# A decoder layer in split fp32 products: few keys' weights scaled three times for one transpose per head, the values' weights split among the keys, and a row sum moved ahead

## The chip, the core and the metric

The kernel runs on one core of one Trainium2 chip. The metric is device time in us, the median of several runs of the program. The engines are TensorE (PE: matmuls, transposes, with a queue PEld that loads the stationary operand), VectorE (DVE), ScalarE (ACT), GpSimd (POOL) and SyncE (SP, which here issues transfers). Each engine works through its own instructions in a fixed order and waits by semaphores.

## The reference

One layer over T = 272 tokens (16 meta tokens ahead of 256) of width D = 2048:

```python
p = h @ w_in                      # q (8 heads x 128) | c_kv (256) | q_idx (16 x 64) | k_idx (64) | w_idx (16) | u (1024)
c_kv = rms_norm(c_kv, g)
score = einsum(relu(q_idx . k_idx), w_idx)      # causal; each query keeps its 64 best keys
logits = (q absorbed by w_uk) . c_kv * 128**-0.5 + T5 bias      # of the keys kept
attn = softmax(logits) @ c_kv, then through w_uv per head
pool = (trailing means of u over 2, 4, 8, 16 minus u) @ w_pool per group, scaled
h = layer_norm(alpha * h + concat(attn, pool) @ w_o)
z = causal depthwise conv of width 3 over h @ w_up
out = layer_norm(alpha * h + (gelu(a) * g) @ w_down)      # a, g the halves of z; meta tokens dropped
```

All inputs and the output are fp32.

## The kernel before

**Products.** Every fp32 factor is held as two parts, hi (an ACT copy rounded to fp32r, L127) and lo (the rest, a DVE subtraction, L128). Each product is three matmuls into one PSUM bank: hi·hi, hi·lo and lo·hi (L199 to L201 in `product`, and the like elsewhere).

**Weights.** They come as a `stream` of tiles of 1 MB, in the order of use. `emit` (L135) takes the next: `fetch` (L110) issues its transfer on SP and splits it in two halves of 1024 columns on ACT and DVE. `weights` (L165) hands out the next tile after it has emitted two more ahead of it (three raw buffers, three split ones). `behind` and `tc.issue_after` add edges to the program, by which an instruction is issued behind another on its engine. The rest of the order is the framework's scheduler's: it puts the instructions of each engine in a fixed order. PSUM has two pools of four banks: `small()` (shown as `at`) and `big()` (shown as `mm`).

**The stages,** with their place in the profiled span:

1. *Warm-up* (L85 to L89): POOL sets a bf16 tile, then 13 matmuls on it. They write nothing that is used.
2. *First products* (L264 to L270): index key, index weights and latent KV, 16 slices k, each split as it lands (L222 to L225). Three PSUM tiles ("heads"), for each k three matmuls for one, then for the next.
3. *Index queries* (to about 82 us): eight products; ACT and DVE evict each into a query tile (L383, L384). `dots` (L352) multiplies it with the key (L358, L359), ACT applies relu from PSUM, DVE adds up the weighted scores.
4. *Keys and values* (75 to 93 us): eight keys `kt` = w_uk times the latent (L398 to L400, evicted on ACT at L401), the last dots among them at key 2; then `few` and the values `v0` (first 16 keys), `v1`, `v2` from w_uv (L409 to L439). `few` holds hi and lo of the latent of the first 16 keys in rows 0 and 32 of a stationary operand of 48 columns, so one product gives both; `v0` has 80 rows: hi, lo and hi again at 0, 32 and 64.
5. *Heads* (138 to 211 us): the products of q and the pool channels. For each head a softmax (L489), `turn` (L504), which transposes the weights (three of 128x128 and, for the first 16 keys, two of 128x16, L506 to L510) and builds `ptx` with the rows hi, hi, lo of these few keys' weights, and `values` (L523). The 16 meta tokens' last two queries have their own small softmax (L463 to L483, tile `lm`), transposed by eight small transposes.
6. *Output product, layer norm, FFN* (to about 1009 us): w_o, w_up and w_down, in part with sums of four blocks in the place of eight products.
7. *Tail* (L895 to L1016): the last four tiles of w_down are applied, `spare` (split tile `whl_y`), `spare` + 1, `spare` + 2 (both `whl`) and the last, which is fetched and split ahead of them into small tiles `whl_r`. Each is taken column by column, in `pieces` of 512 or 256, the one from 1792 to 2048 with two more columns. These hold the row sums of the weights, so that the mean of the second layer norm comes out of the same product. `row_sums` (L185): ACT copies a raw tile onto itself with an accumulated sum (L188), rounds it (L190), DVE takes the rest (L191). Those of `spare`, + 1 and + 2 run behind the split of `spare` + 2, and so do the sums of y (L915). The y adds (L843) close the last parts of the FFN's products.

In the profile L991 to L993 are the tail's matmuls, L785 to L787 and L837 to L839 the FFN's.

## Time and profile before

| what | value |
|---|---|
| median of 3 runs | 1043.34 us (1043.13 to 1043.67) |
| profiled execution | 1043.2 us, of which 1041.3 are the profile's span |
| granted TensorE clock | 0.998 |
| busy: PE, DVE, ACT, POOL | 1033.3, 891.0, 621.0, 189.5 us |
| matmuls | 7643 |
| read from HBM | 232.50 MB, 225 GB/s over the span |

A timeline row has the start (us from the span's start), the busy time, the engine, the line, the operation, output<-input, the shapes and how many instructions it holds; in brackets the idle time just before and what ended it. Consecutive matmuls overlap: a start to the next start is the time that one takes from PE, not its duration. A row of a group has busy us and mean ns of one, then the idle time before it. In the list of waits the numbers are us in total, times, and the longest.

### The profile page before, as it was taken

Reading aid. Unit: us, or ns where it says so; the run is one execution under the profiler, and the core shown is the slowest. Engines: PE = TensorE matmul, PEld = TensorE weight load, DVE = VectorE, ACT = ScalarE, POOL = GpSimd, SP = SyncE. Lnnn points to the kernel's source line nnn. Section 1 sums busy time; section 2 is a strip of 40 time slices with the busy share of each in tenths; the row PEclk is TensorE's granted clock in tenths of the full one; section 3 lists DMA queues with packets and bytes.
Section 4 is the critical chain, followed back from the end, with each engine's and each line's share of the span. In section 5 each row is a group of like instructions: output and inputs, shape, how many; then the busy total and the mean of one; then the engine's idle time right before and its main releaser. Section 6 shows DMA issues by size and latency. Waiting matters only on the chain.

```text
span 1041.3 us, 19198 instructions
## 1 busy us (share of the span) xinstructions
PE 1033.3 (99%) x7643; PEld 984.3 (95%) x7643; DVE 891.0 (86%) x1401; ACT 621.0 (60%) x1000; POOL 189.5 (18%) x246
## 2 busy tenths in 40 slices
PE   9999999999999999999999999999999999999997
PEld 9999999999999999999999999999999999999986
DVE  6879568758779998888999999989998999999876
ACT  7656446645439855555665556555556565565665
POOL 1200014125330021130121111211112101120031
PEclk9999999999999999999999999999999999999999
DMA  9755543354553578879887788877988778887865
GB/s 326 259 187 218 214 142 131 134 200 165 176 189 131 197 223 240 278 282 302 274 277 261 269 297 276 276 263 267 296 271 285 264 274 285 279 273 271 288 215 160
DMA packets 59754, 250.28 MB, mean 240 GB/s; under 512 B 21734, under 2 KB 22416, under 8 KB 32656
## 3 DMA queue, kind: packets, MB, share of 16 engines
q1 hardware_dynamic: 34592, 230.42, 61.2%
q0 software_dynamic: 7888, 16.14, 8.3%
q10 hardware_dynamic: 17184, 2.49, 1.4%
q8 instruction: 60, 0.98, 0.4%
q14 instruction: 30, 0.25, 0.1%
HBM read 232.50 MB, written 2.11 MB: 225 GB/s over the span
## 4 chain that ended last, share of the span: by engine, by line
PE 89%; DVE 5%; issue 3%; ACT 1%; POOL 1%; DMA 1%; POOLq 0%; DVEq 0%; ACTq 0%
PE mm L200 22%; PE mm L199 22%; PE mm L201 22%; PE at L786 6%; PE at L785 6%; PE at L787 6%; DVE whl L128 2%; DMA wraw<-in_w_down 1%; PE mm L268 1%; PE mm L269 1%; PE mm L270 1%; ACT whl L127 1%; DVE x L701 0%; DVE hp L706 0%; PE at L358 0%
## 5 line engine op out<-in xcount | busy, mean ns | idle before, releaser
L128 DVE TENSOR_TENSOR whl<-wraw,whl 128x1024 fp32r<-128x1024 f32 (+1 forms) x416 | 486.3, 1203 | 37.7 <-ACT whl L127 36.8
L127 ACT ACTIVATE whl<-wraw 128x1024 fp32r<-128x1024 f32 (+1 forms) x416 | 402.8, 1015 | 98.6 <-PE mm L201 21.7
L200 PE MATMUL mm<-hp,whl 128*128 128x258 f32 x1280 | 362.4, 283 | 0.1
L199 PE MATMUL mm<-hp,whl 128*128 128x258 f32 x1280 | 361.4, 282 | 0.0
L201 PE MATMUL mm<-hp,whl 128*128 128x258 f32 x1280 | 361.2, 282 | 0.0
L200 PEld LDWEIGHTS mm<-hp,whl 128*128 128x128 f32 x1280 | 242.7, 190 | 3.3 <-DVE hp L706 0.3
L199 PEld LDWEIGHTS mm<-hp,whl 128*128 128x128 f32 x1280 | 242.5, 189 | 3.3
L201 PEld LDWEIGHTS mm<-hp,whl 128*128 128x128 f32 x1280 | 242.9, 190 | 0.2
L199 PE MATMUL mm<-xp,whl 128*128 128x256 f32 (+5 forms) x384 | 111.9, 291 | 0.0
L200 PE MATMUL mm<-xp,whl 128*128 128x256 f32 (+5 forms) x384 | 108.7, 283 | 0.0
L201 PE MATMUL mm<-xp,whl 128*128 128x256 f32 (+5 forms) x384 | 108.7, 283 | 0.0
L720 ACT ACTIVATE z<-mm,cv 128x256 f32<-128x256 f32 x40 | 22.6, 564 | 100.9 <-PE mm L201 100.9
L757 POOL TENSOR_TENSOR forms<-za 128x128 f32<-128x128 f32 x20 | 21.9, 1095 | 309.6 <-DVE za L738 243.1
L720 ACT ACTIVATE za<-mm,cv 128x256 f32<-128x256 f32 x40 | 22.6, 565 | 85.5 <-PE mm L201 77.4
L199 PEld LDWEIGHTS mm<-xp,whl 128*128 128x128 f32 x384 | 72.4, 189 | 1.0 <-issue 0.5
L200 PEld LDWEIGHTS mm<-xp,whl 128*128 128x128 f32 x384 | 72.3, 188 | 0.4
L201 PEld LDWEIGHTS mm<-xp,whl 128*128 128x128 f32 x384 | 72.4, 189 | 0.3 <-DVE whl L128 0.2
L786 PE MATMUL at<-whl,gp 128*128 128x512 f32 x180 | 71.1, 396 | 0.0
L787 PE MATMUL at<-whl,gp 128*128 128x512 f32 x180 | 71.0, 395 | 0.0
L785 PE MATMUL at<-whl,gp 128*128 128x512 f32 x180 | 69.3, 395 | 0.0
L760 POOL TENSOR_TENSOR forms<-za 128x128 f32<-128x128 f32 x20 | 22.6, 1131 | 199.0 <-DVE za L738 185.4
L787 PEld LDWEIGHTS at<-whl,gp 128*128 128x128 f32 x180 | 33.8, 188 | 7.9
(348 smaller groups left out, 1918.2 us busy)
## 6 DMA issues: line engine op xcount, KB each, us to landing
wraw<-in_w_up SPq DMA_DIRECT2D x88, 1024.0 KB, 5.0
wraw<-in_w_down SPq DMA_DIRECT2D x80, 1024.0 KB, 6.2
wraw<-in_w_proj SPq DMA_DIRECT2D x24, 1024.0 KB, 5.1
wraw<-in_w_o SPq DMA_DIRECT2D x16, 1024.0 KB, 4.9
y<-v POOLq DMA_DIRECT2D x27, 256.0 KB, 8.2
y<-u POOLq DMA_DIRECT2D x18, 256.0 KB, 4.9
wraw<-in_w_first SPq DMA_DIRECT2D x8, 304.0 KB, 5.4
x<-in_xt SPq DMA_DIRECT2D x1, 2176.0 KB, 8.4
```

The lines of the kernel that those rows point to most:

```text
L127: upper = nc.scalar.activation(hl[:, 0, c], raw[:, c], AF.Copy)
L128: lower = nc.vector.tensor_tensor(hl[:, 1, c], raw[:, c], hl[:, 0, c].bitcast(F32), op=ALU.subtract)
L199: nc.tensor.matmul(ps, wh, ah, start=n == 0, stop=False)
L200: nc.tensor.matmul(ps, wh, al, start=False, stop=False)
L201: nc.tensor.matmul(ps, wl, ah, start=False, stop=n == KT - 1)
L268: nc.tensor.matmul(ps[:m, :T], wh, x_parts[k][:, 0, :], start=k == 0, stop=False)
L720: nc.scalar.activation(z, src[:, 2:NQ], AF.Identity, bias=col(C_B, j), scale=col(C_W, 3 * j + 2))
L757: nc.gpsimd.tensor_tensor(s[:, 0], a21, a22, op=ALU.add)
L760: nc.gpsimd.tensor_tensor(s[:, 3], a11, a21, op=ALU.subtract)
L785: nc.tensor.matmul(ps, a[:, 0, i], hl[:, 0, w], start=j == 0, stop=False)
L786: nc.tensor.matmul(ps, a[:, 0, i], hl[:, 1, w], start=False, stop=False)
L787: nc.tensor.matmul(ps, a[:, 1, i], hl[:, 0, w], start=False, stop=j == n - 1)
```

## The change

Six edits, all in one kernel; the products and their order on PE stay as they were but for what is named here.

1. **Start.** The warm-up reads a constant of ones in the place of a tile that POOL sets, with 14 matmuls for 13. In the first products the three PSUM tiles' hi·hi go first for k < 4, then their hi·lo, then their lo·hi.
2. **Values' weights.** w_uv is fetched by its turn in the stream but not split there; its raw and split tiles are kept in `held`. Its two halves are split behind the evictions of keys 1 and 3. The evictions of the keys are issued behind the last query's. The last dots use the big PSUM buffers. The tile after w_uv in the stream, the first of the heads' products, is split where w_uv was.
3. **Few keys' values.** `few` has 48 dense columns (hi, hi, lo), `v0` has 112 rows; ACT writes 32 rows at once, POOL copies 48 rows to 64.
4. **Few keys' weights.** The softmax scales the weights of the first 16 keys apart, three copies side by side into a tile `fews` for both blocks of queries (48 columns each, at 0 and 64), so one transpose of 112 columns takes the place of two. The result's parts are formed by row: `lower_row` is 1 for the rows that are to hold lo and 0 for the others; ACT copies with scale 1 − 2·lower_row, so hi or −hi, and DVE adds lower_row times the full value.
5. **Meta queries' weights.** `lm3` holds three copies of `lm` (two DVE copies), eight transposes of 48 columns for 16; the parts in the same way, in `pm_parts`, from which POOL copies two columns per head into `ptx`.
6. **Tail.** The row sum of `spare` is issued when `spare` + 1 is emitted, behind `spare`'s split and ahead of `spare` + 1's. The two others follow the split of `spare` + 2 as before; the sums of y are issued behind them.

By the programs' orders, DVE now does both last y adds (L843; L887 in the changed kernel) between the low halves of `spare` + 1 and those of `spare` + 2; before, it did one ahead of each of the latter's two. On PE one matmul of the tail's second piece goes ahead of the first that needs the low half of `spare` + 2. PE has 8 transposes fewer and one warm-up matmul more. SP's transfers and their order are the same.

```diff
-    warm = sb.tile([P, 256], mybir.dt.bfloat16, name="warm")
-    nc.gpsimd.memset(warm, 0.0)
+    warm = nc.const_aps.tensor(1.0, (P, 256), mybir.dt.bfloat16)
     ps = small()
-    for _ in range(13):
+    for _ in range(14):
...
+    def split_part(raw, hl, c, after=()):
+        with ExitStack() as edges:
+            for ins in after:
+                edges.enter_context(tc.issue_after(ins))
+            upper = nc.scalar.activation(hl[:, 0, c], raw[:, c], AF.Copy)
+        lower = nc.vector.tensor_tensor(hl[:, 1, c], raw[:, c], hl[:, 0, c].bitcast(F32), op=ALU.subtract)
+        return tuple(getattr(ins, "ins", ins) for ins in (upper, lower))
...
+        if i == VALUES:
+
+            nc.sync.dma_start(raw, stream[i])
+            held.extend((raw, hl))
+            return
+        if i == spare + 1:
+
+            with behind(spare):
+                sums = row_sums(spare, ready[spare])
+            split[i] = fetch(raw, hl, stream[i], None, 0, (sums,))
...
+        terms = [(t, h) for h in heads for t in range(3)]
+        if k < 4:
+            terms.sort(key=lambda x: x[0])
...
-        nc.scalar.activation(kt[:, h, :], ps[:, :T], AF.Copy)
+        with tc.issue_after(query):
+            key = nc.scalar.activation(kt[:, h, :], ps[:, :T], AF.Copy)
         if h == 2:
-            dots(7, qis[7], small(), (0, 1))
+            dots(7, qis[7], big(), (0, 1), big)
+        if h in (1, 3):
+
+            split_part(*held, slice(512 * h - 512, 512 * h + 512), (getattr(key, "ins", key),))
...
+        nc.scalar.activation(v[:32, w], ps[:32], AF.Copy)
+        nc.vector.tensor_tensor(low, ps[:NM], v[:NM, w].bitcast(F32), op=ALU.subtract)
+        nc.vector.tensor_tensor(low, ps[32:48], low.bitcast(F32), op=ALU.add)
+        nc.gpsimd.tensor_copy(v[64:FEW, w], v[:48, w])
...
+    def stacked_parts(to, ps, r):
+
+        nc.scalar.activation(to, ps, AF.Copy, scale=lower_row[r:r + 48, 1:2])
+        nc.vector.scalar_tensor_tensor(to, ps, lower_row[r:r + 48, 0:1], to.bitcast(F32), op0=ALU.mult, op1=ALU.add)
...
-            nc.vector.tensor_scalar_mul(lg[:, a:b], lg[:, a:b], st[:, 2, i:i + 1])
+            nc.vector.tensor_scalar_mul(lg[:, a + NM:b], lg[:, a + NM:b], st[:, 2, i:i + 1])
+            nc.vector.tensor_scalar_mul(fews[h % 2][:, 64 * i:64 * i + 48].rearrange("p (a b) -> p a b", b=NM),
+                                        lg[:, None, a:a + NM].to_broadcast([P, 3, NM]), st[:, 2, i:i + 1])
...
-        nc.tensor.transpose(ptm[:NM, :P], lg[:, :NM], ident)
-        nc.tensor.transpose(ptm[:NM, P:2 * P], lg[:, KA:KA + NM], ident)
+        nc.tensor.transpose(ptm[:FEW, :P], fews[h % 2], ident)
...
-        for r in (0, 32):
-            nc.vector.tensor_copy(ptx[r:r + NM, :2], pm_sb[:, h, :])
-            nc.scalar.activation(ptx[r:r + NM, 2:], ptm[:NM, :2 * P], AF.Copy)
-        nc.vector.tensor_tensor(ptx[64:64 + NM, :2], pm_sb[:, h, :], ptx[:NM, :2].bitcast(F32), op=ALU.subtract)
-        nc.vector.tensor_tensor(ptx[64:64 + NM, 2:], ptm[:NM, :2 * P], ptx[:NM, 2:].bitcast(F32), op=ALU.subtract)
+        nc.gpsimd.tensor_copy(ptx[:48, :2], pm_parts[:, h, :])
+        for i in range(2):
+            stacked_parts(ptx[64 * i:64 * i + 48, 2 + P * i:2 + P * i + P], ptm[64 * i:64 * i + 48, :P], 64 * i)
...
     with behind(spare + n - 2):
-        for k in range(n - 1):
-            row_sums(spare + k, hls[k])
+        for k in range(1, n - 1):
+            of_weights = row_sums(spare + k, hls[k])
...
     for i in range(2):
-        nc.scalar.activation(y2[:, i], y2[:, i], AF.Copy, accum_out=mvs[i][:, 0:1])
+        with tc.issue_after(of_weights):
+            nc.scalar.activation(y2[:, i], y2[:, i], AF.Copy, accum_out=mvs[i][:, 0:1])
```

More of the change, by code (lines that the diff above doesn't have):

```diff
@@ L154, in emit @@
             raw, hl = weight_tiles()
[L155 removed]
         ready[i] = hl
+        if i == VALUES:
[6 more added lines that the diff above has]
+            split[i] = fetch(raw, hl, stream[i], None, 0, (sums,))
+        else:
+            split[i] = fetch(raw, hl, stream[i], kinds.get(i), i and i - 1 in split and split[i - 1][1])
         if i >= spare:
```

92 lines of the change are left out of this document (50 added, 42 removed).

## The prediction

> **What bounds the kernel now.** I read the busy times on the page first, then the chain that ended last by engine, then what TensorE (PE) sat idle for.
>
> ```profile
> PE 1033.3 (99%) x7643; PEld 984.3 (95%) x7643; DVE 891.0 (86%) x1401; ACT 621.0 (60%) x1000; POOL 189.5 (18%) x246
> ...
> PE 89%; DVE 5%; issue 3%; ACT 1%; POOL 1%; DMA 1%; POOLq 0%; DVEq 0%; ACTq 0%
> ```
>
> And PE's list of waits, whole (us in total, times, longest):
>
> ```profile
> PE at L975 <- ACT diag L973: 1.5, 1, 1.5
> PE at L89 <- POOL warm L86: 1.1, 1, 1.1
> PE mm L992 <- DVE whl L191: 0.2, 1, 0.2
> ```
>
> PE is busy 99% of a span of 1041.3 us, and its list of waits holds 2.8 us in all (1.5 + 1.1 + 0.2). So the change can win only what it takes from PE's own work, or from short stalls that this list counts as busy. It can lose without such a bound: each us by which an operand is late for PE is a us of the end. I therefore follow PE's starts, and ask at each touched place whether the next start comes earlier or later. The usual pace is 0.12 us for 258 columns (1018.89 to 1019.01 in the last fence of this part) and by its columns 0.125 for 272 and 0.23 to 0.24 for 512.
>
> **The change, part by part**
>
> *Start.* The warm-up loses its wait for POOL's memset, gets a 14th matmul, and the first four k take all three heads' hi·hi products first.
>
> ```profile
> 1.10 2.95 PE L89 MATMUL at<-warm 128*128 128x256 bf16 x13 [1.10 <-POOL warm L86]
> ...
> 5.96 0.33 PE L270 MATMUL mm<-xp,whl 128*128 128x272 f32 x1
> ...
> 8.36 0.43 ACT L222 ACTIVATE xp<-wraw 128x272 fp32r<-128x272 f32 x1 [0.96 <-DMA wraw<-in_w_first]
> ...
> 9.20 0.51 DVE L225 TENSOR_TENSOR whl<-wraw,whl 128x336 fp32r<-128x336 f32 x1
> ...
> 9.76 0.35 PE L270 MATMUL mm<-xp,whl 128*80 128x272 f32 x1
> 9.95 0.29 PE L268 MATMUL mm<-xp,whl 128*128 128x272 f32 x1
> ```
>
> Products run at half pace until about 5.96. But at 9.76 PE takes the fifth k's low half of the weights, which VectorE (DVE) ends at 9.20 + 0.51 = 9.71; that one came through ScalarE (ACT) from a transfer that ACT had awaited until 8.36. The next start is at 9.95, 0.19 later where the pace is 0.125: PE is already waiting for data there, by some 0.06 us. Whatever it wins before 9.7 is spent in this wait, which only grows. I cost the whole edit at 0; the cover is the transfer behind 8.36. What PE loses before 9.7 isn't covered, since it has no slack there. The full pace comes 4.86 us after the first warm matmul (5.96 − 1.10). If it came 2 us later by the clock, 2 us more at half pace would cost 1 us. Bounds: −0.1 to +1.
>
> The Trainium skill, "TensorE: Matmul & The Clock Gate", section "What's actually happening", says that the clock is released by a free-running window of about 3.4 us of activity, and that the number of cold matmuls differs from run to run. The trace's 4.86 us fits one such window begun at a phase of its own. By that rule a start that is earlier on PE need not release the clock earlier, and this can go either way; my sum has 0 here by the row at 9.20, whichever holds.
>
> *Values' weights split among the keys; last dots in the big buffers.* The rows of PE, then of ACT and DVE, around 80 us:
>
> ```profile
> 80.09 0.28 PE L200 MATMUL mm<-xp,whl 128*128 128x258 f32 x1
> 80.39 0.39 PE L201 MATMUL mm<-xp,whl 128*128 128x258 f32 x1
> 80.62 0.28 PE L199 MATMUL mm<-xp,whl 128*128 128x258 f32 x1
> 81.04 0.39 PE L358 MATMUL at<-kidx,qi 128*128 128x272 f32 x1
> 81.27 0.29 PE L359 MATMUL at<-kidx,qi 128*128 128x272 f32 x1
> ...
> 85.71 0.39 PE L426 MATMUL at<-whl,few 128*48 128x512 f32 x1
> ```
>
> ```profile
> 79.51 1.06 ACT L127 ACTIVATE whl<-wraw 128x1024 fp32r<-128x1024 f32 x1
> 80.59 0.98 ACT L401 ACTIVATE kt<-at 128x272 f32<-128x272 f32 x3
> 81.44 0.31 ACT L361 ACTIVATE rl<-at 128x144 f32<-128x144 f32 x1
> ```
>
> ```profile
> 79.11 1.23 DVE L128 TENSOR_TENSOR whl<-wraw,whl 128x1024 fp32r<-128x1024 f32 x1 [0.53 <-ACT whl L127]
> 80.37 0.43 DVE L384 TENSOR_TENSOR qi<-mm,qi 64x256 fp32r<-64x256 f32 x1
> ```
>
> From 80.09 to 81.27 PE makes four steps in 1.18 us where 0.485 would do: a hidden stall of **0.70 us**. It waits for the low half of the next projection's weights (DVE 79.11 + 1.23 = 80.34), then for a PSUM buffer: the small ones hold keys that ACT evicts only at 80.59, behind the split at 79.51 that takes 1.06. In the changed order that projection is split some 6 us earlier, two keys go ahead of the first half of the values' weights, and the dots take buffers of the other pool. So both reasons go. What is late next is the relu of the first head's dots, which frees nothing before it has gone through ACT. ACT's order is then: second query (behind no split now, it ends at an estimated 78.9), two keys (2 × 0.33, to 79.5), half a split (1.0, to 80.5), a key (0.33) and the relu (0.31, to about 81.1); PE without a stall could go on at 80.97: 0.16 us of it stays. Gain 0.70 − 0.16 = **−0.53** (rounded); bounds −0.2 (a second wait of 0.3) and −0.76 (no stall at all, and the short steps around). The second half of the values' low parts comes at about 84.5 and PE, which multiplies with it at 85.71 now, wants it at about 85.3 once the stall is shorter, so 0.8 us covers the later split; if DVE were late by more, the excess would be paid.
>
> For the first values (48 stacked rows) PE keeps eight matmuls. ACT loses two of its four copies, POOL gets two of 48x512; their reader is the first head's product at 151.6 (quoted next), over 60 us later.
>
> *One transpose per head.* PE's product that reads the new tile, then PE's start of the first head and what DVE does around it:
>
> ```profile
> L526 PE MATMUL at<-ptx,v x8: 279/284/287, 151.6 to 209.3; 80*128 80x258 f32 x8
> ```
>
> ```profile
> 145.37 0.34 PE L482 MATMUL at<-ident,lm 2*16 2x2 f32 x8
> 145.65 0.33 PE L506 MATMUL at<-ident,lg 128*128 128x128 f32 x1
> ...
> 146.03 0.27 PE L509 MATMUL at<-ident,lg 128*16 128x128 f32 x1
> 146.14 0.27 PE L510 MATMUL at<-ident,lg 128*16 128x128 f32 x1
> ```
>
> ```profile
> 144.84 0.27 DVE L476 TENSOR_TENSOR lm<-lm,mmeta 2x128 f32<-2x128 f32 x1
> ...
> 145.82 0.15 DVE L483 COPY pm_sb<-at 16x16 f32<-16x16 f32 x1
> ```
>
> A transpose lasts 0.27 us, but the next starts 0.11 later (146.03 to 146.14): they overlap, and one less per head is worth 0.109 us, eight times **−0.87**. The first head alone gets something ahead: DVE has two more copies of 2x128 (0.15 each by the copy at 145.82) and two narrow scalings, which by the rows end near 145.6 where PE wants to start at 145.6: 0 to +0.1. On DVE the softmax's scalings get narrower (128 and 256 columns for 144 and 272) and two of 128x48 join; three tiny copies and one of 256 columns become two of 128: about even. ACT's two copies have 128 columns for 256. POOL's extra copy of 48x2 per head stands right behind its memset, ahead of the pool's windows; it takes 0.15 us or so, and PE reads the tile at 151.6, 5 us after the first head's transposes. I take −0.87, bounds −0.95 to +0.1.
>
> The Trainium skill, "TensorE: Matmul & The Clock Gate", section "Part 4: PE-mode transpose", gives about 275 ns for a transpose in a kernel. The trace's duration agrees (0.27), its starts don't (0.11); by the page's figure as a cost, eight would be an estimated 2.2 us.
>
> *The row sum in ACT's gap.* PE's stall that it is aimed at, and ACT's and DVE's tail:
>
> ```profile
> 1011.88 0.39 PE L992 MATMUL mm<-whl,gp 128*128 128x512 f32 x1
> ...
> 1018.89 0.28 PE L993 MATMUL mm<-whl,gp 128*128 128x258 f32 x1
> 1019.01 0.28 PE L991 MATMUL mm<-whl,gp 128*128 128x258 f32 x1
> 1019.49 0.39 PE L992 MATMUL mm<-whl,gp 128*128 128x258 f32 x1 [0.20 <-DVE whl L191]
> 1019.72 0.28 PE L993 MATMUL mm<-whl,gp 128*128 128x258 f32 x1
> ```
>
> ```profile
> 1006.43 2.02 ACT L127 ACTIVATE whl<-wraw 128x1024 fp32r<-128x1024 f32 x2 [2.83 <-DMA wraw<-in_w_down]
> ...
> 1014.67 1.90 ACT L188 ACTIVATE wraw<-wraw 128x2048 f32<-128x2048 f32 x1
> ...
> 1018.55 0.19 ACT L190 ACTIVATE whl<-total 128x2 fp32r<-128x2 f32 x1
> ```
>
> ```profile
> 1002.69 2.36 DVE L128 TENSOR_TENSOR whl_y<-wraw,whl_y 128x1024 fp32r<-128x1024 f32 x2 [1.95 <-ACT whl_y L127]
> ...
> 1009.81 0.68 DVE L843 TENSOR_TENSOR y<-y,mm 128x512 f32<-128x512 f32 x1
> 1010.40 1.22 DVE L128 TENSOR_TENSOR whl<-wraw,whl 128x1024 fp32r<-128x1024 f32 x1
> ```
>
> The last matmuls wait for the last total (1018.55 + 0.19, then DVE): 1018.89 to 1019.72 hold 0.83 us where three steps need 0.36, so 0.47 us go. In their place: the moved sum writes over the raw tile, so it waits for DVE's last low half of that tile, 1002.69 + 2.36 = 1005.05. It takes 1.90 as its like at 1014.67, and with its read-out and the two columns' copy (0.19 a row, partly overlapped) 2.15 or so; the next tile's split, now issued behind it, starts at about 1007.2 instead of 1006.43. DVE's two low halves of that tile then run 8.32 to 10.6 (us past 1000). In the changed order DVE does both adds to y next (0.60 each from start to start, 9.81 to 10.40), to 11.8, and only then the last tile's first low half (1.22): ready at 1013.02. Before, one add stood ahead of it and it was ready at 1011.62 for PE's 1011.88. One matmul that is moved ahead gives 0.23, so PE comes to it at 1012.10: a **new stall of 0.92**, with the semaphore's way 0.97. Net tail −0.47 + 0.97 = **+0.50**. Bounds: −0.47 (the tile comes early enough) and +1.5 (another us from the transfer or from the adds, which wait for PE). The remaining sums run on ACT behind the last split as before, one fewer of them, and PE asks for their totals at 1019.49 only.
>
> **Sum**: 0 − 0.53 − 0.87 + 0.50 = **−0.90**. DVE's rows that stand in between don't absorb it, since PE's chain is continuous through the FFN. The profiled execution took 1043.2 (span 1041.3 and 1.9 around it): 1042.3. The median of the runs shown is 1043.34, 0.14 above it, which gives **1042.4**.
>
> **The rivals**
>
> *A. The tail does as it is meant.* If the last tiles are ready a us earlier than I work out, or PE comes a us later to them, the new stall is nothing: −0.53 − 0.87 − 0.47 = −1.87, 1041.5. For it: the whole stall hangs on 1 us between three engines. Against: DVE's order is fixed, and 8.32 + 2.3 + 1.2 + 1.2 is a sum of measured durations. With the keys' stage at its other bound too (−0.76) it is 1041.2, just faster.
>
> *B. The moved sum delays the splits by more, slower.* Place: ACT between 1005 and 1009. The sum decides when the low half of the tile ahead of it is later than about 1004.2 (1006.43 − 2.2); from there each us costs PE one. With that transfer's landing 3.2 us later, the stall would be 4.2 and the sum −0.53 − 0.87 − 0.47 + 4.2 = +2.3: 1045.6. Against: its start at 1002.69 follows from a stream that is ahead of PE here.
>
> *C. The stall among the dots only moves* (the change doesn't do what it says): the relu or the values' low half takes the place of the split, and 0.7 stays: −0.87 + 0.50 = −0.37, 1043.0.
>
> *D. A dropped transpose gives back its duration* of 0.27, not the distance of 0.11, because PE can't overlap one with the matmul behind it: 8 × 0.27 = 2.16 for 0.87, so −2.19 in all: 1041.15. The starts at 146.03 and 146.14 speak against it. [...]
>
> *E. The clock comes later at the start*, up to +1: 1043.4.
>
> **How the numbers follow.** A measurement of this kernel can tell about 0.2%, 2.1 us, from no change, so faster means below 1041.25 and slower above 1045.4. Forecast 0.46; A 0.23, of which 0.08 lie below the bound; B 0.06, of which 0.04 lie above; C 0.14; D 0.03, all faster; E 0.08, 0.01 of it slower. Faster: 0.08 + 0.03 + 0.02 from the forecast's own spread = 0.13; slower 0.05; same 0.82. The range takes in A, C, D and E: from 1040.9 (A with the keys' −0.76, the heads' −0.95 and the start's −0.1 gives 1041.1, and 0.2 for the median's own scatter) to 1044.1 (the tail at +1.5 and the keys at −0.2 give 1043.8, and a third of E). What is left out is B and a later mix of the losses, some 1 in 10 to 2 in 10.
>
> **What would show it.** Right: between 79.9 and 81.3 PE's steps are 0.12 but for one; one transpose of 112 rows a head, its neighbour 0.11 later; the matmul at 1019.49 follows without a gap; PE has a gap of about 1 us near 1012, waiting for DVE's low half, behind two adds. Wrong: no gap there (then A); a gap above 2 us (B); PE waits for ACT's relu or DVE's low half between 80 and 86 (C); PE at half pace beyond 6.5 us (E); PE waits for the stacked weights' tile in any head, which I cost at nothing.

## The result and the profile after

The changed kernel takes 1047.40 us (median of 6 executions, 1046.95 to 1049.11) against 1043.62 for the kernel before, run beside it: ratio **1.0039, interval 1.0028 to 1.0049**. That is some 4 us slower, where 0.9 us faster was forecast and 1044.1 was the upper end of the range. The profiled execution took 1047.3, of which 1045.5 are the span; the granted clock is 0.998 as before.

The page of the changed kernel, busy times and then the chain that ended last by engine:

```profile
PE 1033.1 (99%) x7636; PEld 983.3 (94%) x7636; DVE 893.5 (85%) x1406; ACT 620.7 (59%) x999; POOL 191.2 (18%) x257
...
PE 82%; DVE 9%; issue 3%; ACT 2%; DMA 1%; POOL 1%; SPq 0%; POOLq 0%; DVEq 0%; ACTq 0%
```

PE is busy for 0.2 us less than before, in a span that is 4.2 us longer. So PE's work hardly changed and its waiting did; in the chain DVE's share rose from 5% to 9%. Among PE's waits (us in total, times, longest) three are new, beside one of 1.2 us in the start:

```profile
PE at L615 <- DVE mixa L575: 2.2, 2, 1.3
...
PE mm L1037 <- DVE whl L116: 0.9, 1, 0.9
...
PE at L556 <- DVE mixp L621: 0.7, 1, 0.7
```

`mixa` (two waits) and `mixp` are all among the heads; the whl of L1037 is the tail's wait that was forecast. What PE waits for in them is no data but a PSUM bank: DVE's subtraction into `mixa` (or `mixp`) is the last to read a head's result (or a pool group's) from a small bank, and PE's next product into that bank can't start before it. No term of the prediction names these.

**Where the 4.1 us come from.** I split the span at points that both kernels have. The heads go from the first product of the meta queries' logits to the first FFN product, before and then after:

```profile
139.01 0.45 PE L466 MATMUL at<-kt,qt 128*2 128x16 f32 x12
...
350.12 0.28 PE L199 MATMUL mm<-hp,whl 128*128 128x258 f32 x1
```

```profile
138.96 0.50 PE L494 MATMUL at<-kt,qt 128*2 128x16 f32 x14
...
352.85 0.28 PE L219 MATMUL mm<-hp,whl 128*128 128x258 f32 x1
```

211.11 us became 213.89: **+2.78**, where −0.87 was forecast. Ahead of them the two kernels are even (139.01 and 138.96). Behind them 0.63 us are lost in the FFN with no wait to be seen (measured below), and the tail, up to its last product, loses 0.75 (0.82 up to the span's end).

**The heads' first wait.** PE, before and after, at a pool product between the heads, which needs such a bank:

```profile
171.49 0.28 PE L571 MATMUL at<-df,wpl 128*128 128x258 f32 x1
```

```profile
170.82 0.28 PE L617 MATMUL at<-df,wpl 128*128 128x258 f32 x1
172.37 0.39 PE L615 MATMUL at<-df,wpl 128*128 128x258 f32 x1 [1.27 <-DVE mixa L575]
```

By its pace PE would have gone on at 170.94 (170.82 + 0.12) and it does at 172.37: 1.43 us lost. Two more follow, 1.06 at 190.5 and 0.90 at 205.8. Now ACT some 7 us earlier, before and after:

```profile
163.91 0.74 ACT L518 ACTIVATE ptx<-at 16x256 fp32r<-16x256 f32 x2
...
165.27 2.00 ACT L127 ACTIVATE whl<-wraw 128x1024 fp32r<-128x1024 f32 x2
```

```profile
164.50 0.35 ACT L521 ACTIVATE ptx<-at,lower_row 48x128 fp32r<-48x128 f32 x1
...
165.63 0.36 ACT L521 ACTIVATE ptx<-at,lower_row 48x128 fp32r<-48x128 f32 x1 [0.47 <-DVE ptx L522]
...
166.44 2.01 ACT L115 ACTIVATE whl<-wraw 128x1024 fp32r<-128x1024 f32 x2
```

Before, ACT's two copies into `ptx` ran back to back. Now the second waits for DVE's addition into the first's half of the same tile. The bracket shows only 0.47 us of waiting, but it is a wait across two queues: that addition stands behind what DVE does ahead of it. DVE, after:

```profile
165.09 0.26 DVE L547 TENSOR_SCALAR few_of<-lg,st 128x48 f32<-128x48 f32 x1
165.26 0.33 DVE L522 SCALAR_TENSOR_TENSOR ptx<-at,lower_row,ptx 48x128 fp32r<-48x128 f32 x1
...
167.53 2.94 DVE L116 TENSOR_TENSOR whl<-wraw,whl 128x1024 fp32r<-128x1024 f32 x2 [1.15 <-ACT whl L115]
...
171.90 0.42 DVE L575 TENSOR_TENSOR mixa<-at,mixa 128x258 fp32r<-128x258 f32 x1
```

And `mixa` before:

```profile
170.80 0.41 DVE L531 TENSOR_TENSOR mixa<-at,mixa 128x258 fp32r<-128x258 f32 x1
```

Read them in order: the addition ends at 165.59, so ACT's second copy at 165.63, so its weight split at 166.44 and not at 165.27 (+1.17), so DVE's low half, which had waited 1.15 for it, at 167.53, so the subtraction into `mixa` at 171.90 and not at 170.80 (+1.10). Before, `mixa`'s subtraction freed the bank at 171.21 for PE's 171.49: a margin of **0.28 us**. PE itself comes 0.55 earlier (170.94 for 171.49): four transposes are dropped by then, 4 × 0.109 = 0.44, and it began 0.05 earlier. 1.10 + 0.55 − 0.28 = 1.37 of the 1.43. So at this place the other engines, not PE, set the pace, though PE is busy 99% of the span.

POOL has a part in this chain too. Its windows (the trailing sums of the pool channels) read a tile that ACT writes behind the second copy, so they also end a us later. POOL, before and after:

```profile
166.22 2.18 POOL L553 TENSOR_TENSOR win<-win 128x263 f32<-128x263 f32 x2
```

```profile
167.20 2.19 POOL L597 TENSOR_TENSOR win<-win 128x263 f32<-128x263 f32 x2
```

DVE's last low half ends some 1.1 us behind them in both: 166.35 + 3.14 = 169.49 behind 168.40 before, 170.47 behind 169.39 after. Whether ACT's split or POOL's windows made it late can't be told from these two kernels; the next runs say more.

**The tail.** PE, then DVE, then ACT, after:

```profile
1015.22 0.39 PE L1036 MATMUL mm<-whl_y,gp 128*128 128x512 f32 x1
1016.50 0.50 PE L1037 MATMUL mm<-whl,gp 128*128 128x512 f32 x1 [0.90 <-DVE whl L116]
```

```profile
1006.14 2.36 DVE L116 TENSOR_TENSOR whl_y<-wraw,whl_y 128x1024 fp32r<-128x1024 f32 x2 [2.02 <-ACT whl_y L115]
...
1014.03 1.28 DVE L887 TENSOR_TENSOR y<-y,mm 128x512 f32<-128x512 f32 x2
1015.23 2.35 DVE L116 TENSOR_TENSOR whl<-wraw,whl 128x1024 fp32r<-128x1024 f32 x2
```

```profile
1008.53 1.92 ACT L207 ACTIVATE wraw<-wraw 128x2048 f32<-128x2048 f32 x1 [1.48 <-DVE whl_y L116]
1010.68 3.90 ACT L115 ACTIVATE whl<-wraw 128x1024 fp32r<-128x1024 f32 x4
```

The moved sum starts when DVE ends `whl_y`'s low half (1006.14 + 2.36 = 1008.50), and the next split comes 2.15 later. Two additions stand ahead of the last low half on DVE, and PE waits for that: step 1.28 where 0.23 is the pace. The old wait for the last total is gone: at the product that had it PE's step is now 0.12. All of this is as forecast.

### The profile page after: what moved, and what is told of

It reads as the page before. It is cut to its first block, busy times and chain, and to the rows that moved or that the text cites. A ratio compares the mean times of both kernels' runs of the same rounds, so it can differ in the third digit from the quotient of the medians.

```text
span 1045.5 us, 19194 instructions
## 1 busy us (share of the span) xinstructions
PE 1033.1 (99%) x7636; PEld 983.3 (94%) x7636; DVE 893.5 (85%) x1406; ACT 620.7 (59%) x999; POOL 191.2 (18%) x257
## 3 DMA queue, kind: packets, MB, share of 16 engines
HBM read 232.50 MB, written 2.11 MB: 224 GB/s over the span
## 4 chain that ended last, share of the span: by engine, by line
PE 82%; DVE 9%; issue 3%; ACT 2%; DMA 1%; POOL 1%; SPq 0%; POOLq 0%; DVEq 0%; ACTq 0%
PE mm L220 20%; PE mm L219 20%; PE mm L221 20%; PE at L829 6%; PE at L830 6%; PE at L831 6%; DVE whl L116 4%; PE mm L291 2%; DMA wraw<-in_w_down 1%; ACT whl L115 1%; ACT lg L543 0%; DVE x L745 0%; DVE hp L750 0%; DVE lg L546 0%; DVE lg L539 0%
## 5 line engine op out<-in xcount | busy, mean ns | idle before, releaser
L801 POOL TENSOR_TENSOR forms<-za 128x128 f32<-128x128 f32 x20 | 21.2, 1061 | 311.9 <-DVE za L782 245.3
L804 POOL TENSOR_TENSOR forms<-za 128x128 f32<-128x128 f32 x20 | 19.8, 990 | 200.0 <-DVE za L782 200.0
```

Source lines behind the costliest of these rows:

```text
L801: nc.gpsimd.tensor_tensor(s[:, 0], a21, a22, op=ALU.add)
L804: nc.gpsimd.tensor_tensor(s[:, 3], a11, a21, op=ALU.subtract)
```

## The experiments

Each kernel was run with the kernel before on the same chip; the ratio has its 95% interval. "Heads" is the length from the first to the second mark above, less the 211.11 of before. "FFN" is measured in the same way between two rows quoted with the reversed turn. Both come from one profiled execution of each kernel; the ten kernels that have the heads of before lie within 0.07 us of it.

| kernel | median us | ratio to before | heads | FFN |
|---|---|---|---|---|
| changed | 1047.40 | 1.0039 (1.0028 to 1.0049) | +2.78 | +0.63 |
| e1 heads as before | 1044.75 | 1.0011 (1.0003 to 1.0020) | −0.04 | +0.63 |
| e2 copies first | 1045.25 | 1.0017 (1.0008 to 1.0026) | +0.61 | +0.65 |
| e4 heads' edits alone | 1046.52 | 1.0029 (1.0017 to 1.0040) | +2.74 | 0.00 |
| e7 the wait alone | 1046.48 | 1.0030 (1.0018 to 1.0041) | +3.17 | 0.00 |
| e13 e2, small copy on DVE | 1046.74 | 1.0027 (1.0016 to 1.0037) | +2.82 | +0.63 |
| e15 e2, scalings on POOL | 1047.57 | 1.0039 (1.0025 to 1.0053) | +0.85 | +0.63 |
| e16 e4, copies first, scalings on POOL, big dots | 1044.52 | 1.0020 (1.0011 to 1.0028) | +2.83 | 0.00 |
| e5 e2, y adds late | 1044.13 | 1.0006 (0.9997 to 1.0015) | +0.14 | +0.63 |
| e9 e1, y adds late | 1044.23 | 1.0003 (0.9994 to 1.0012) | −0.06 | +0.63 |
| e10 start alone | 1043.72 | 1.0000 (0.9991 to 1.0009) | 0.00 | 0.00 |
| e14 start and tail, adds late | 1043.51 | 0.9999 (0.9990 to 1.0008) | +0.01 | 0.00 |
| e8 split and big dots alone | 1043.84 | 1.0000 (0.9991 to 1.0009) | −0.06 | +0.63 |
| e11 big dots alone | 1043.40 | 0.9994 (0.9985 to 1.0004) | +0.01 | +0.01 |
| e12 split alone | 1043.97 | 1.0004 (0.9995 to 1.0013) | −0.04 | +0.64 |
| e17 turn reversed alone | 1044.26 | 1.0008 (0.9999 to 1.0017) | −0.06 | +0.63 |
| e18 e12, turn put back | 1044.06 | 1.0005 (0.9997 to 1.0014) | 0.00 | 0.00 |
| e19 e9, turn put back | 1043.21 | 0.9992 (0.9983 to 1.0001) | +0.01 | 0.00 |
| e20 e5, turn put back | 1043.53 | 0.9995 (0.9986 to 1.0004) | +0.56 | +0.01 |

### The heads

My theory on seeing the traces: the wait between ACT and DVE in `ptx` costs the heads. The rival: it is the added work on DVE (or on POOL), and the wait is only where it shows.

**e1**: the heads and the few keys' values as before, the rest of the change kept.

```diff
-            nc.vector.tensor_scalar_mul(fews[h % 2][:, 64 * i:64 * i + 48]...
-        nc.tensor.transpose(ptm[:FEW, :P], fews[h % 2], ident)
+        nc.tensor.transpose(ptm[:NM, :P], lg[:, :NM], ident)
+        nc.tensor.transpose(ptm[:NM, P:2 * P], lg[:, KA:KA + NM], ident)
```

> The changed kernel with everything that concerns the few keys put back (stacked latent of 48 columns with gaps, values of 80 rows, one small softmax copy, two transposes per head, the copies into the tile ptx as before); start, split of the values' weights among the keys, and tail stay changed. By the trace of the changed kernel against before, PE is level with before when the heads start (139.3 in both) and 2.8 us late after them (212.2 against 209.4), and 4.1 late at its last product. Theory (the heads' part costs 2.8): about 1044.6, no gaps of a us on PE between 165 and 206 us. Rival (the stalls among the heads come from what is ahead of them, the values' weights being split later): the gaps stay, about 1047.

**e2**: the change, with both copies ahead of both additions, so that ACT waits for DVE in no head.

```diff
-        for i in range(2):
-            stacked_parts(ptx[64 * i:64 * i + 48, 2 + P * i:2 + P * i + P], ptm[64 * i:64 * i + 48, :P], 64 * i)
+        for to, low, sign in ends:
+            nc.scalar.activation(to, low, AF.Copy, scale=sign[:, 1:2])
+        for to, low, sign in ends:
+            nc.vector.scalar_tensor_tensor(to, low, sign[:, 0:1], to.bitcast(F32), op0=ALU.mult, op1=ALU.add)
```

> The changed kernel with one edit: in each head both ScalarE copies into ptx stand ahead of both VectorE additions, so the second copy no longer waits for the first addition. Nothing else is moved or left out. Theory 1 (the wait: ScalarE's second copy waits for VectorE, which first scales the next head's weights, and the weight split behind it is late by 0.5 us a head until PE has to wait): the three stalls on PE (1.4, 1.1, 0.9 us) go, about 1044.0, and the profile has ACT idle for less than 0.1 ahead of the second copy. Theory 2 (VectorE's own added work, two more scalings of 128x48 a head, makes it late): the stalls stay within a third, 1046.5 or more. Theory 3 (GpSimd's copy of 48x2, 0.8 us, holds ptx back): no change, 1047.4.

**e4**: the kernel before with the few keys' edits alone, parts 3 to 5 of the change (and the constant of ones with 13 matmuls).

```diff
-        nc.tensor.transpose(ptm[:NM, :P], lg[:, :NM], ident)
-        nc.tensor.transpose(ptm[:NM, P:2 * P], lg[:, KA:KA + NM], ident)
+        nc.tensor.transpose(ptm[:FEW, :P], fews[h % 2], ident)
```

> The kernel before with only the few keys' part of the change (and the warm-up's constant tile in the place of the one that GpSimd sets, to make room; 13 matmuls). Start order, values' weights, tail as before. If the heads' part costs its 2.8 us by itself: 1043.5 + 2.8 = 1046.3, with stalls on PE between 165 and 206. If it does so only together with the values' weights' later split: 1043.5 - 0.9 = 1042.7.

**e7**: the kernel before, its operations all kept and only put in an order that makes ACT's second copy wait for DVE.

```diff
-            nc.scalar.activation(ptx[r:r + NM, 2:], ptm[:NM, :2 * P], AF.Copy)
...
+        nc.scalar.activation(ptx[:NM, 2:], ptm[:NM, :2 * P], AF.Copy)
         nc.vector.tensor_tensor(ptx[64:64 + NM, 2:], ptm[:NM, :2 * P], ptx[:NM, 2:].bitcast(F32), op=ALU.subtract)
+        nc.scalar.activation(ptx[32:32 + NM, 2:], ptm[:NM, :2 * P], AF.Copy)
```

> The kernel before with one edit in each head: the second ScalarE copy into ptx stands behind VectorE's subtraction that ends ptx, so ScalarE waits there for VectorE, as in the changed kernel; the work is the same. Theory 1 (that wait is the cost): slower, about 1045.5, with PE stalls of 0.5 to 1.5 us among the later heads. Theory 2 (the added work): 1043.5 within 0.5.

With the heads undone (e1) their length is that of before and 2.65 us of the median go (1047.40 to 1044.75). The heads alone (e4) cost the same on the kernel before. The wait alone (e7), with no work added anywhere, costs 3.17 in the heads; and without it (e2) 2.17 of the 2.78 go, 2.15 by the medians. So the cost of ACT's wait is shown from both sides, for 2.2 us of it. PE's waits in e7, those among the heads:

```profile
PE at L572 <- DVE mixa L532: 1.6, 2, 0.8
PE at L509 <- DVE mixp L578: 0.8, 1, 0.8
```

They are at the same three places as in the changed kernel. ACT's copies and its split in e2:

```profile
164.40 0.73 ACT L565 ACTIVATE ptx<-at,lower_row 48x128 fp32r<-48x128 f32 x2
...
165.88 2.00 ACT L115 ACTIVATE whl<-wraw 128x1024 fp32r<-128x1024 f32 x2
```

The copies are back to back again. But counted from the first mark (138.72 here) the copies come 0.78 later than in the kernel before (25.68 us for 24.90) and the split 0.90 later (27.16 for 26.26), and one wait of PE for `mixa` stays, a step of 1.41 us over the pace. It is the first of the three: 1.43 in the changed kernel, and it ends 33.41 us after the first mark in both. So the order of the copies costs the second wait and the third. The first stays without it, though that order alone is enough for a wait there too (0.94 in e7). 0.61 − 1.41 = −0.80: the transposes do give what was forecast (−0.87), and the wait that is left takes it away and more. For that rest the rival may hold: the added work on DVE is in the groups of the changed kernel's heads (busy us, mean ns of one, idle time ahead):

```profile
L522 DVE SCALAR_TENSOR_TENSOR ptx<-at,lower_row,ptx 48x128 fp32r<-48x128 f32 x16 | 5.5, 347 | 2.7 <-ACT ptx L521 2.5
L547 DVE TENSOR_SCALAR few_of<-lg,st 128x48 f32<-128x48 f32 x16 | 4.1, 254 | 0.0
```

Those that they replace, in the kernel before:

```profile
L520 DVE TENSOR_TENSOR ptx<-at,ptx 16x256 fp32r<-16x256 f32 x8 | 3.3, 410 | 0.1
L517 DVE CAST ptx<-pm_sb 16x2 fp32r<-16x2 f32 x16 | 2.5, 154 | 0.2
L519 DVE TENSOR_TENSOR ptx<-pm_sb,ptx 16x2 fp32r<-16x2 f32 x8 | 1.2, 152 | 0.3
```

The additions and the copies for the few keys take 5.5 + 4.1 us for 3.3 + 2.5 + 1.2: 2.6 us more, or 0.33 a head, on a loop with 0.28 us of margin. Narrowing the wide scaling from 272 to 256 columns saved nothing (370 ns for 354).

Three tries to take the rest of e2's wait away. **e13** has POOL's copy of 48x2 on DVE, **e15** the two narrow scalings on POOL, **e16** is e4 with the copies first, these scalings on POOL and the big dots.

```diff
-        nc.gpsimd.tensor_copy(ptx[:48, :2], pm_parts[:, h, :])
+        nc.vector.tensor_copy(ptx[:48, :2], pm_parts[:, h, :])
```

```diff
-            nc.vector.tensor_scalar_mul(fews[h % 2][:, 64 * i:64 * i + 48]...
+            nc.gpsimd.tensor_scalar_mul(fews[h % 2][:, 64 * i:64 * i + 48]...
```

> The changed kernel with both ScalarE copies first in each head, and the copy of two columns (48x2) per head made by VectorE in the place of GpSimd. With the copies first, one stall of 1.4 us was left at 170.6 us, where PE waits for VectorE's subtraction of the third head's mix. Theory A (what is left is VectorE's own added work, 0.24 us a head by its starts): the stall grows, to 1.6 to 2, since VectorE gets 0.1 us more per head; 1045.4. Theory B (GpSimd's copy is what is left: it delays the windows that VectorE waits for): the stall falls under 0.7; 1044.5.

> The changed kernel with both ScalarE copies first in each head, and the two scalings of 128x48 per head made by GpSimd in the place of VectorE. With the copies first alone, 1.4 us of stall was left at 170.6 us and the kernel took 1045.25. Theory (VectorE's added scalings, 0.34 us a head by their starts, are what is left): the stall falls under 0.6, and the heads' stage is shorter than before's 211.1 us by 0.3 or more; 1044.3. Rival (GpSimd's work delays its windows, or holds VectorE, by as much): the stall stays above 1.2, 1045.2 or more.

> The kernel before with the few keys' part (copies first, the narrow scalings on GpSimd), the warm-up's constant tile, and the last dots in the big buffers; values' weights and tail as before. A candidate for a version better than both. Theory: 1043.6 - 0.3 (dots) - 0.4 (heads) = 1042.9. Rival (a stall among the heads takes it back): 1043.6 or more.

None did: the one step is 2.15 in e13, 1.73 in e15 and 2.11 in e16. In e15 DVE now waits 0.27 us for POOL's scalings.

What is left of the wait has POOL's windows in its chain. DVE in e2, ahead of the second head's `mixa` and then in the third head, and POOL there:

```profile
162.43 0.43 DVE L606 SCALAR_TENSOR_TENSOR diff<-win,u 128x258 f32<-128x258 f32 x1 [0.73 <-POOL win L600]
...
166.97 3.26 DVE L116 TENSOR_TENSOR whl<-wraw,whl 128x1024 fp32r<-128x1024 f32 x2 [0.57 <-ACT whl L115]
```

```profile
166.97 2.18 POOL L600 TENSOR_TENSOR win<-win 128x263 f32<-128x263 f32 x2
```

The second head's windows end 0.79 us later after the first mark than in the kernel before (23.68 us for 22.89), DVE waits 0.73 for them, and ACT's copies come the 0.78 late that was seen above. The third head's windows end 30.43 us after the mark, as in the changed kernel (29.39 before). DVE's last low half again ends 1.08 behind them, although it began 0.32 earlier after the mark than in the changed kernel. e5 has e2's heads and a step of 0.94. POOL and DVE in e5:

```profile
167.34 3.27 POOL L600 TENSOR_TENSOR win<-win 128x263 f32<-128x263 f32 x2
```

```profile
167.35 2.79 DVE L116 TENSOR_TENSOR whl<-wraw,whl 128x1024 fp32r<-128x1024 f32 x2 [0.57 <-ACT whl L115]
```

In both kernels the two engines start within 0.01 us of each other. In e2 DVE takes 0.47 more than in e5; in e5 POOL takes 1.09 more than in e2. One holds up the other, which of them differs, and PE's steps differ by the same 0.47 (1.41 and 0.94; e20, where DVE is held up, has 1.35). So the first wait passes through POOL's windows. How much of their lateness comes from DVE's added work the runs don't split, and that stays open.

That e13's and e16's heads are nearly 3 us longer with a single wait of 2.15 and 2.11 has a further cause, which e13's profile shows by stretches of time (us, then busy us and count of PE, PEld, DVE, ACT, POOL, then the granted clock, DMA share, GB/s):

```profile
172.00:176.00 4.00, 2.01 (x17) 1.80 (x16) 3.53 (x11) 1.97 (x7) 0.00 (x0) 1.00 0.55 180
176.00:179.50 3.50, 3.50 (x19) 3.50 (x18) 2.74 (x9) 3.16 (x8) 0.90 (x2) 0.51 0.30 104
```

```profile
174.71 0.39 PE L618 MATMUL at<-df,wpl 128*128 128x258 f32 x1 [1.99 <-DVE mixa L578]
```

After an idle time of 1.99 us PE runs at full clock for 1.3 us more, and then at 0.51 for about 3.4 us: a step of 0.22 for 0.12, some 1.5 us lost. −0.87 + 2.15 + 1.5 = 2.78, of 2.82. e16 shows the same behind 1.95 us. In e15's profile (1.57) and the changed kernel's (1.27) the clock stays at 1.00. The profiled executions of e13 and e16 were above their medians (1048.61 of 1046.74; 1047.33 of 1044.52), so it is probably not met every time. e15's other executions (1047.57 to 1048.56 for three of five, the profiled one 1045.59) may be of that kind; that wasn't seen in a profile.

### The tail and the start

**e5** is e2, and **e9** is e1, with the last y adds behind the low halves of `spare` + 2. **e14** is the kernel before with the start and the tail's edits, adds late; **e10** has the start alone.

```diff
-                    nc.vector.tensor_tensor(yc, yc, downs[i], op=ALU.add)
+                    with tc.issue_after(split[spare + 2][1]) if end else ExitStack():
+                        nc.vector.tensor_tensor(yc, yc, downs[i], op=ALU.add)
```

> The changed kernel with both ScalarE copies first in each head (as in the run before) and, in the tail, both last additions to y issued behind the low halves of the last-but-one tile's successor, so that VectorE no longer does them ahead of it. Theory (the new stall of the tail, 1.1 us near 1013 us, is the two additions ahead of that low half): PE waits less than 0.3 us there, and neither stall of the tail is left; 1045.2 - 1.1 = 1044.1. Rival (the low half is late because ScalarE's row sum pushes its split): the stall stays above 0.7, 1045.2.

> The changed kernel with the few keys' part put back as before, and the last additions to y behind the last low halves. Neither stall of the tail, none among the heads. Theory: 1043.5 - 0.4 (dots) - 0.5 (tail) = 1042.6, plus up to 0.6 by the slower pace between 360 and 980 us if that belongs to the start, the dots or the tail: 1042.6 to 1043.2. Rival (what is won ahead of the heads or in the tail is lost in another wait): 1043.5 or more.

e10, and with it e14:

```diff
+    warm = nc.const_aps.tensor(1.0, (P, 256), mybir.dt.bfloat16)
-    for _ in range(13):
+    for _ in range(14):
...
+        if k < 4:
+            terms.sort(key=lambda x: x[0])
```

> The kernel before with only the start and the tail changed, the tail with its last additions to y behind the last low halves: the candidate for a version better than both. Theory: the tail's stall of 0.47 us goes, no other comes, no loss of pace: 1043.6 - 0.5 = 1043.1. Rival (the row sum in ScalarE's gap or the late additions cost elsewhere in the tail): 1043.6 or more.

> The kernel before with only the start changed (constant of ones, 14 warm-up matmuls, hi by hi first for k < 4). Theory (the first products wait for their transfers in either order): 1043.5 within 0.4; PE waits for the weights of k = 1 or k = 4, at a place that the transfers' landing sets. Rival (the earlier clock is kept): 1043.0. If the slower pace between 360 and 980 us comes with it, 1044.1.

The tail's stall, 1.16 in the changed kernel, is 0.26 in e5, none in e9 and 0.69 in e14. DVE in e5:

```profile
1009.27 4.66 DVE L116 TENSOR_TENSOR whl<-wraw,whl 128x1024 fp32r<-128x1024 f32 x4 [0.79 <-ACT whl L115]
```

All four low halves now go ahead of the adds, which begin at 1013.85. So the two adds are what makes the last tile late, as the prediction worked out. The tail is then worth little either way. e9, without the stall, was expected at 1042.6 to 1043.2 and took 1044.23 (1.0003); e14, with part of it, was expected at 1043.1 and took 1043.51 (0.9999). The start alone is 1.0000; forecast at 0.

### The dots, and 0.63 us with no wait

**e8** is the kernel before with the values' split among the keys and the big buffers for the last dots; **e11** has the buffers alone, **e12** the split alone. The split, then the buffers:

```diff
+        if h in (1, 3):
+            split_part(*held, slice(512 * h - 512, 512 * h + 512), (getattr(key, "ins", key),))
...
         if h == 2:
-            dots(7, qis[7], small(), (0, 1))
+            dots(7, qis[7], big(), (0, 1), big)
```

> The kernel before with only the values' weights split among the keys and the last dots in the big buffers. Theory: the stall of 0.70 us near 80 us falls to 0.3 as in the changed kernel; but before had only 0.28 us between VectorE's last subtraction of the third head's mix (171.2) and PE's need of its buffer (171.5), so of the gain hardly 0.3 is left: 1043.3, or 1043.9 if the pace of the long products that follow (0.1% slower in every kernel with the changed base) comes from this part. Rival (the gain at 80 us is kept whole): 1043.1.

> The kernel before with one edit: the last query's dots take their three PSUM tiles from the big buffers in the place of the small ones, which also moves the turn of the four banks of each pool for all that follows. Seen so far: in the six kernels that hold the dots' part, PE loses 0.6 us between 359 and 977 us against before, in the three others nothing. Theory (the banks' turn makes the long products slower): that 0.6 us appears here, 1043.6 + 0.6 - (what is left of the stall at 80 us, up to 0.3) = 1043.9 to 1044.2. Rival (it comes from the tiles of the values' weights): no change of pace, 1043.3 to 1043.6.

> The kernel before with the values' weights split among the keys and the keys' evictions behind the last query's, the last dots in the small buffers as before. Theory of the banks' turn: no loss of pace between 359 and 977 us, and the stall at 80 us shorter than 0.7 by what the earlier evictions give: 1043.2 to 1043.6. Rival: the 0.6 us of pace is here, 1043.9 or more.

The forecast gain at the dots is there: of a stall of 0.69 us 0.30 is left, and 0.38 with the small buffers. PE, after:

```profile
81.17 0.29 PE L421 MATMUL at<-ctp,whl 128*128 128x272 f32 x1
81.48 0.38 PE L380 MATMUL mm<-kidx,qi 128*128 128x256 f32 x1
```

But e8 is no faster, since every kernel with the split lost 0.63 us between 359 and 977 us, evenly and without a wait. e11 rules out the turn of the PSUM buffers, which I had first suspected. The split has another side effect: the values' tile is out of the row of splits, and from there on the three buffers of split tiles are used in the reverse turn (2 1 0 before, 0 1 2 now, as the programs have it; the traces leave buffer numbers out). **e17** is the kernel before with only that: tile 12 is fetched in its turn but split behind tile 13. **e18** is e12 with the same exchange, which puts the turn back.

```diff
+        if i == 12:
+            nc.sync.dma_start(raw, stream[i])
+            held.extend((raw, hl))
+            return
...
+        if i == 12 + 1:
+            split[12] = fetch(*held, stream[12], None, 0, False)
```

> The kernel before with one edit that has nothing to do with the values: one projection tile (number 12 of the stream) is fetched in its turn, but its split is written behind that of the next, so that from there on the three buffers of the weights' tiles are used in the reverse turn, the same as in the changed kernel. Theory (the turn is the cause): PE loses 0.6 us against before between 359 and 977 us. Rival: no loss there. The time itself also holds what the swapped splits cost near 100 us.

> The kernel with only the values' weights split among the keys (last dots in the small buffers), with the same swap of one later projection tile, which puts the turn of the buffers back to that of before. Theory (the turn is the cause): no loss against before between 359 and 977 us. Rival (something else of that split is): the loss of 0.6 us stays.

The first and the last of a row that all have, before, e17 and e18:

```profile
358.84 0.55 ACT L720 ACTIVATE za<-mm,cv 128x256 f32<-128x256 f32 x1
...
977.46 0.57 ACT L720 ACTIVATE za<-mm,cv 128x256 f32<-128x256 f32 x1 [2.34 <-PE mm L201]
```

```profile
360.09 0.55 ACT L727 ACTIVATE za<-mm,cv 128x256 f32<-128x256 f32 x1
...
979.35 0.57 ACT L727 ACTIVATE za<-mm,cv 128x256 f32<-128x256 f32 x1 [3.05 <-PE mm L208]
```

```profile
359.88 0.55 ACT L746 ACTIVATE za<-mm,cv 128x256 f32<-128x256 f32 x1
...
978.49 0.57 ACT L746 ACTIVATE za<-mm,cv 128x256 f32<-128x256 f32 x1 [2.41 <-PE mm L222]
```

618.62 before, 619.26 with the turn reversed alone, 618.61 with the split and the turn put back. So the turn is the cause. Why a turn of SBUF buffers costs PE one part in a thousand is open. The medians alone (1.0008 and 1.0005) don't tell these two apart; the rows do.

### Put together

**e19** is e9 and **e20** is e5, each with the turn put back by the same exchange at tile 18.

```diff
+            if i == 18:
+                nc.sync.dma_start(raw, stream[i])
+                later.extend((raw, hl))
+                return
...
+            if i == 18 + 1:
+                split[18] = fetch(*later, stream[18], None, 0, (), False)
```

> The changed kernel with the few keys' part put back, the last additions to y behind the last low halves, and the turn of the weights' buffers put back (tile 18 of the stream is split behind tile 19). Theory (turn, tail and heads' part are all that cost): no loss of pace between 359 and 977 us, the span 0.6 us under that of the same kernel without the last edit (1041.1): 1042.9. Rival (the swapped split makes PE wait by as much among the heads): 1043.5 or more.

> The whole change with three edits: both ScalarE copies first in each head, the last additions to y late, the turn of the weights' buffers put back. Without the last edit it took 1044.13. Theory: 1044.13 - 0.6 = 1043.5, level with before. Rival (the stall at the third head grows by what comes earlier): 1044 or more.

e19 (heads as before) is at 0.9992, 0.9983 to 1.0001, e20 at 0.9995, 0.9986 to 1.0004: neither is measurably faster than before. e20's heads are still 0.56 longer than before's, because of the wait that is left.

## Why the prediction was wrong, by its steps

- **Heads, −0.87: failed, measured +2.78.** The step reads "On DVE the softmax's scalings get narrower … about even. ACT's two copies have 128 columns for 256." It weighed the busy time of each engine, and neither their order nor the PSUM banks that DVE frees. In the order copy, add, copy, add ACT waits for DVE's add behind four scalings, and three waits of PE follow, 1.43 + 1.06 + 0.90 = 3.39; 3.39 − 0.87 = 2.52, and some 0.26 stay spread over short steps. By e2 this order costs the second wait and the third, 2.17 of the heads' time. The first stays without it: it passes through POOL's windows, and what DVE's added work has to do with it stays open. The transposes' price itself (0.109 each) was right, by e2's −0.80; rival D (0.27 each) fell. "About even" was off by 0.33 us a head, more than the 0.28 of margin, and where ACT's wait is gone (e2) the heads still cost +0.61. The prediction named what would show it ("PE waits for the stacked weights' tile"), but the wait came somewhere else: at a bank that DVE frees, which is late because DVE, ACT and POOL are late by then.
- **What let it fail:** the prediction says that each us by which an operand is late for PE is lost, but in the heads it asked this of the reader of `ptx` alone, which had 5 us of cover, and of no bank. The row that spoke against it was in the trace of before: the bank of `mixa` free at 171.21 for PE's 171.49. It bounded the heads at +0.1.
- **Dots, −0.53: right in mechanism, −0.40 measured.** 0.30 is left where 0.16 was worked out.
- **Tail, +0.50: right in mechanism, +0.75 measured.** The 2.15 from the sum's start to the next split came out at 2.15; the new stall was 1.05 for 0.97, with 0.11 more in a second step. The reading rests on these rows more than on the 0.75, since nine kernels that left the tail as it was differ from before by −0.49 to +0.30 over the same stretch. Rival A fell (the stall is there), and so did B (it stays near 1 us, and the time is past B's for another reason).
- **Start, 0: right.** e10 is 1.0000. In the changed kernel PE waits 0.99 us for the second slice's weights, not the fifth's as the prediction had it, and that wait takes up whatever came earlier.
- **FFN, not in the sum: +0.63.** No step looked at which buffer each later tile gets.
- **Rival C** fell: the dots' gain is kept. **E** was not seen: PE has its full pace from 3.8 us on, earlier than before. The 4.1 us of the profiles are −0.05 up to the heads (+0.32 in the first products, by when their transfers land, −0.40 at the dots, the rest rounding and small steps), +2.78, +0.63 and +0.75.

## What to carry to other kernels

An engine that is busy 99% of the span is the bound on average; whether a gain on it can be kept is read, stage by stage, from how long each of its operands was ready, and each of its PSUM banks free, before it was wanted. Where an edit splits one copy and one add into two of each on two engines, write all copies ahead of all adds: interleaved, the second copy inherits the other engine's queue, and everything behind it on its own engine is late too. A wait can have two causes, each of them enough: with one of them gone (e2) the first wait was as long as before. An edit that takes one tile out of a turn of buffers moves all that come after it, so look at a stretch far behind it as well.

## What the runs showed of the hardware that was not expected

- **Half clock after a wait.** 1.95 to 1.99 us without a matmul (e16, e13) were followed by about 3.4 us at a granted clock of 0.51, which began 1.3 us after PE had started again. The Trainium skill, "TensorE: Matmul & The Clock Gate", section "What's actually happening", has the half clock after an idle window of some 3.4 us, free-running. The length agrees; the idle time needed doesn't, as 2 us were enough here. No bound follows for the idle time alone: 1.57 us in e15's profile left the clock at 1.00, while behind the tail's wait of 1.49 us in e20, with few products around it, it is 0.50.
- **POOL beside DVE.** The 48x2 copy takes 0.18 us in one head and over four times that in another. POOL, and then DVE, in the changed kernel:

```profile
162.81 0.18 POOL L562 CAST ptx<-pm_parts 48x2 fp32r<-48x2 f32 x1
...
169.70 0.81 POOL L562 CAST ptx<-pm_parts 48x2 fp32r<-48x2 f32 x1
```

```profile
168.83 1.64 DVE L116 TENSOR_TENSOR whl<-wraw,whl 128x1024 fp32r<-128x1024 f32 x1
```

  The long one ends at 170.51, which is 0.04 us behind the end of DVE's subtraction (168.83 + 1.64 = 170.47). The Trainium skill, "SBUF — State Buffer", section "🔬 SBUF: two separate sides", says that these two engines share a pair of ports which one of them holds for its whole instruction; the trace agrees. So do POOL's windows and DVE's low half in e2 and e5 above, of which one is always held up. The prediction had this copy at 0.15.
- **The turn of three SBUF buffers** is worth 0.63 us in 618 (e17, e18), with no wait in the trace.
